# Attention with the softmax weights left unnormalised, and the outputs of two heads divided by rows of their sums

## The chip, the core and the metric

The kernel runs on one core of one Trainium2 chip. The metric is device time in microseconds (us) of one execution of the whole program; the number compared is the median of several. The core has a matrix engine (TensorE, in rows PE, its weight loads PEld), a vector engine (DVE), an activation engine (ACT), GpSimd (POOL) and a queue that only issues transfers (SP). They run side by side, each through its own queue of instructions in order, and wait for one another on semaphores.

## The reference

Two transformer blocks on 1024 tokens of width 1024. The first is a gated delta-net layer with an MLP. The second has, on the same input, softmax attention and a gated linear recurrence, then an output product and a gated MLP. The change is in the attention of the second block:

```
keys = concat([kc, kx])        # 256 context tokens + 1024 tokens = 1280 keys
vals = concat([vc, vx])
# 8 query heads of 64, 2 key/value heads, blocks of 128 queries
s = einsum('bqkgd,bnkd->bkgqn', q, keys) * scale
p = softmax(s, axis=-1)                       # exp(s - max) / sum
o = einsum('bkgqn,bnkd->bqkgd', p, vals)
```

The division by the sum is by query and head, so it may stand before or after the product with the values.

## The kernel before

All matrix products keep fp32 accuracy: each operand is split into a rounded part (`hi`) and a remainder (`lo`), and three (or two) products are added in PSUM.

`attention` works in chunks. A chunk is 128 queries of one head against all 1280 keys. `chunks` lists 64 of them: head pair j (4), half of the tokens i (2), head of the pair h (2), block of 128 queries c (4). So one (j, i) is eight chunks: two heads, four blocks. Two chunks that follow each other make a pair m (32 pairs).

For one chunk `dots` issues six matmuls into a PSUM tile called `logits` (four banks of 512 columns; even chunks use columns 0 to 1279, odd ones 768 to 2047, so that neighbours overlap). DVE takes the row maximum (line 1248). `rest` is the exponential on ACT (line 1252), which writes the weights `w` (128 x 1280) and, by `accum_out`, their sum into a small tile `st`. `norm` is a reciprocal on DVE (line 1255) and a multiplication of the whole tile `w` by it on POOL (line 1256).

The loop over `steps` takes a pair in five steps s of 256 keys. A step turns four 128 x 128 pieces of the pair's two `w` tiles on PE into a PSUM tile from `k.pt()` (line 1336; there are two such buffers), ACT rounds that to `ph` (line 1340), DVE makes the remainder `pl` (line 1345), and `product` multiplies both by the values into `pv` (lines 1323, 1324), three steps later or so. In step 0 of pair m the dots of chunk 2m+3 are issued, in step 2 those of chunk 2m+4; their exponentials follow in the same step, and their `norm` one step later. The pieces of chunk 2m+3 are first turned in step 0 of the next pair. At the end of four chunks `tail` adds the two halves of `pv` (ACT copy to `ao`, line 1266, DVE add to `att`, line 1267). After the second head (h = 1) it sends `att` to memory, or, for j = 3, splits it into `mixed[3]` (lines 1272, 1273).

Into this loop other work is put by `fill`: the projection of the next queries and their norm and rotation (`prep`, whose multiplications are on POOL, lines 1114 to 1129), and a gate (`gate`). In the last fifth, results of the other heads are read back and split on POOL (`split_mixed`, line 1381).

The order on each engine is not simply that of the program. The framework has a planner that takes instructions by their place in the program when their inputs are ready by its own modelled durations, and writes the queues down before the kernel runs. So PE turns the pieces of the pair's first chunk earlier than those of the second where the second comes later, and a `w_out` load of the following stage is issued while the attention has just begun. On the chip each queue is then followed strictly.

After the loop comes the output product (`out_tile`, line 2057): eight tiles over the first half of the tokens, then eight over the second. `mixed[3]` is its last operand.

Of the kernel before, what the change touches and what calls it, by code (L numbers as in the profile page):

```python
# [9 lines left out]
F32 = mybir.dt.float32  # L10
F32R = mybir.dt.float32r
AF = mybir.ActivationFunctionType
ALU = mybir.AluOpType
AX = mybir.AxisListType
# [179 lines left out]
def drain(g):  # L194
    for _ in g or ():
        pass
# [832 lines left out]
def mixer(k, hhi, hlo, mixd, cpd):  # L1029

    nc, tc = k.nc, k.tc
    w_in = k.A["w_in_2"]

    def proj(n, evac, o=0):
        W = k.wload(w_in[:, 128 * n:128 * n + 128])
        for i, sl in enumerate(HALVES):
            ps = k.pg()
            k.gemm(ps, W, hhi, hlo, sl)
            evac(ps, slice(o + 512 * i, o + 512 * i + 512), i)

    k.nh = (hhi, hlo)
    mixed = [None] * 8
    with tc.tile_pool(name="mix", bufs=1, reuse_waits="tile") as P:
        with tc.tile_pool(name="hgr", bufs=1, reuse_waits="tile") as R:
            first = Keys(k, P, cpd)
            hgrn(k, P, R, proj, mixd, cpd, first)
        with tc.tile_pool(name="att", bufs=1, reuse_waits="tile") as R:
            attention(k, P, R, proj, mixd, cpd, mixed, first)
    return mixed
# [110 lines left out]
def attention(k, P, R, proj, mixd, cpd, mixed, first):  # L1160

    nc, A = k.nc, k.A
# [33 lines left out]
                nc.scalar.copy(v[:, :, 0:64], p)  # L1196
                nc.vector.tensor_tensor(out=v[:, :, 64:128], in0=p, in1=v[:, :, 0:64], op=ALU.subtract)

    QT, Q, W, att = {}, {}, {}, {}
    logits = k.psL.tile([128, 2048], F32, name="logits")  # L1200

    def prep(j):
# [23 lines left out]
    def queries(j, i):  # L1226


        ps = k.pt()
        for c in range(4):  # L1230
            nc.tensor.transpose(ps[:, 128 * c:128 * c + 128], QT[j][:, 4 * i + c, :], k.ident)
        for h in range(2):
            QS = Q[j, i, h] = R.tile([128, 512], F32R, tag="QS", name=k.nm("QS"), bufs=4)
            p, o = slice(64 * h, 64 * h + 64), slice(64 * (1 - h), 64 * (1 - h) + 64)
            nc.scalar.copy(QS[p, :], ps[p])
            nc.vector.tensor_tensor(out=QS[o, :], in0=ps[p], in1=QS[p, :], op=ALU.subtract)

    def dots(n):

        j, i, h, c = chunks[n]  # L1240
        g, q = j // 2, Q[j, i, h][:, 128 * c:128 * c + 128]
        o = 768 * (n % 2)
        lg = logits[:, o:o + 1280]
        for a, b in (((0, 512), (512, 1024), (1024, 1280)), ((768, 1280), (256, 768), (0, 256)))[n % 2]:
            nc.tensor.matmul(lg[:, a:b], q, KH[g][:, a:b], start=True, stop=False)
            nc.tensor.matmul(lg[:, a:b], q, KL[g][:, a:b], start=False, stop=True)
        st = R.tile([128, 4], F32, tag="st", name=k.nm("st"), bufs=4)
        nc.vector.tensor_reduce(out=st[:, 0:1], in_=lg, axis=AX.X, op=ALU.max, negate=True)
        w = W[n] = R.tile([128, 1280], F32, tag="w", name=k.nm("w"), bufs=5)

        def rest():
            nc.scalar.activation(w, lg, AF.Exp, bias=st[:, 0:1], accum_out=st[:, 1:2])

        def norm():
            nc.vector.reciprocal(st[:, 2:3], st[:, 1:2])  # L1255
            nc.gpsimd.tensor_scalar(w, w, st[:, 2:3], None, op0=ALU.mult)  # L1256
        return rest, norm

    def tail(j, i, h, pv):

        if h == 0:
            att[j, i] = R.tile([128, 512], F32, tag="att", name=k.nm("att"), bufs=2)
        o, sl = att[j, i], HALVES[i]
        p = slice(64 * h, 64 * h + 64)
        o2 = R.tile([64, 512], F32, tag="ao", name=k.nm("ao"), bufs=1)
        nc.scalar.copy(o2, pv[64:128, :])
        nc.vector.tensor_tensor(out=o[p, :], in0=pv[0:64, :], in1=o2, op=ALU.add)
        if h == 0:
            return
        if j == 3:  # L1270
            hi, lo = mixed[3]
            nc.scalar.copy(hi[:, sl], o)
            nc.gpsimd.tensor_tensor(out=lo[:, sl], in0=o, in1=hi[:, sl], op=ALU.subtract)
        else:
            nc.sync.dma_start(mixd[j][:, sl], o)

    def reload(f):

        mixed[f] = halves(f)
        nc.sync.dma_start(mixed[f][1].bitcast(F32), mixd[f])  # L1280

    def halves(f):
        return tuple(k.s2.tile([128, 1024], F32R, tag="s2", name=f"mx{c}{f}") for c in "hl")

    chunks = [(j, i, h, c) for j in range(4) for i in range(2) for h in range(2) for c in range(4)]
# [8 lines left out]
    def fill(n=1):  # L1294
        for _ in range(n):
            if todo:
                next(todo.pop(0), None)
                if not todo:
                    drain(fills[3])

    def ahead(n):
        return dots(n) if n < len(chunks) else (lambda: None, lambda: None)

    for n in range(3):
        rest, norm = ahead(n)
        rest()
        fill(3)
        norm()

    steps = [(m, s) for m in range(32) for s in range(5)]  # L1310
    waiting, pv = [], None
# [2 lines left out]
    def product(m, s, ph, pl):  # L1314

        nonlocal pv, hold
        j, i, h, c = chunks[2 * m]
        if c == 0 and s == 0:
            pv = k.psV.tile([128, 512], F32, tag="v", name=k.nm("pv"))
        out = pv[:, 128 * c:128 * c + 256]  # L1320
        for e in range(2):
            kt, sl = 2 * s + e, slice(256 * e, 256 * e + 256)
            nc.tensor.matmul(out, V[j // 2][:, kt, :], ph[:, sl], start=kt == 0, stop=False)
            nc.tensor.matmul(out, V[j // 2][:, kt, :], pl[:, sl], start=False, stop=kt == 9)
        if c == 2 and s == 4:
            tail(j, i, h, pv)
            hold = 2

    for n, (m, s) in enumerate(steps):
        if s == 0:  # L1330
            rest, norm = ahead(2 * m + 3)
        ps = k.pt()
        for e in range(2):
            for c in range(2):
                kt = 2 * s + e
                nc.tensor.transpose(ps[:, 256 * e + 128 * c:256 * e + 128 * c + 128],  # L1336
                                    W[2 * m + c][:, 128 * kt:128 * kt + 128], k.ident)
        ph = R.tile([128, 512], F32R, tag="ph", name=k.nm("ph"), bufs=4)
        pl = R.tile([128, 512], F32R, tag="pl", name=k.nm("pl"), bufs=4)
        nc.scalar.copy(ph, ps)  # L1340
        if s in (0, 2):
            if s == 2:
                rest, norm = ahead(2 * m + 4)
            rest()
        nc.vector.tensor_tensor(out=pl, in0=ps, in1=ph, op=ALU.subtract)  # L1345
        if s in (1, 3):
            norm()
        waiting.append((m, s, ph, pl))
        hold -= 1
        if hold < 0 or len(waiting) > 3:  # L1350
            for _ in range(2 if len(waiting) > 3 else 1):
                if len(waiting) > 2:
                    product(*waiting.pop(0))

        nxt = 2 * m + 6
        if s == 3 and nxt % 8 == 0 and nxt < len(chunks):
            j, i = chunks[nxt][:2]
            while j not in QT:
                fill()
            queries(j, i)  # L1360
        if n < 112 and (n * 83) // 108 != ((n + 1) * 83) // 108:
            fill()
        if n == 114:
            drain(fills[3])
            todo.clear()
            drain(fills[2])
            mixed[3] = halves(3)
        for f in {116: (4, 5), 122: (6, 7), 128: (0, 1), 134: (2,)}.get(n, ()):
            reload(f)
        if n in (130, 134, 138, 142, 146, 150, 154):  # L1370
            f = (4, 5, 6, 7, 0, 1, 2)[(n - 130) // 4]
            split_mixed(k, mixed[f], HALVES[0], nc.gpsimd.tensor_copy, nc.gpsimd)
# [5 lines left out]
def split_mixed(k, pair, sl, copy, eng=None):  # L1378
    hi, lo = pair[0][:, sl], pair[1][:, sl]
    copy(hi, lo.bitcast(F32))  # L1380
    (eng or k.nc.vector).tensor_tensor(out=lo, in0=lo.bitcast(F32), in1=hi, op=ALU.subtract)
# [789 lines left out]
```

## Time and profile before

| | us |
|---|---|
| median of 3 runs | 3133.63 (3132.91 to 3140.13) |
| profiled execution | 3129.6, of which the trace's span is 3127.8 |
| attention loop, first maximum to last product | about 1884 to 2325 in the span |
| PE busy in the span | 2840.2 (91%) |
| DVE, ACT, POOL busy in the span | 2131.3, 1402.3, 1075.1 |
| mean granted PE clock in the span | 0.961 |

Times in the rows are us from the start of the span unless they are marked ns. A row of a group of instructions has the source line, the engine, the operation, output<-input by the program's names, and a count; "idle before" is time in which the engine had nothing to do until the named instruction of another engine let it go. PEclk is the granted clock as a share of full speed.

### The profile page before, as it was taken

What the parts mean: (1) busy time and instruction counts of PE and PEld (TensorE: products, weight loads), DVE (VectorE), ACT (ScalarE), POOL (GpSimd) and SP (SyncE); (2) the same over time, 40 slices, a digit from 0 to 9 for tenths busy, and PEclk for the clock granted to TensorE, in tenths of its full rate; (3) what the DMA queues carried; (4) which work ended last, traced back from release to release, by engine and by line L of the source; (5) the groups of instructions that cost most, each with busy time, mean ns of one, the idle gap of its engine ahead of it and who ended that gap; (6) DMA issues with size and microseconds to landing.
All of it is one profiled execution on the core that took longest, in us unless ns stands there. A gap on an engine that the chain in (4) does not pass through costs nothing. (4 is left out here: it accounts for less than half of the span.)

```text
span 3127.8 us, 43961 instructions
## 1 busy us (share of the span) xinstructions
PE 2840.2 (91%) x16304; PEld 2313.7 (74%) x16304; DVE 2131.3 (68%) x3267; ACT 1402.3 (45%) x2677; POOL 1075.1 (34%) x756
## 2 busy tenths in 40 slices
PE   7899999997899989998999997787779899999998
PEld 5777777786677767887777776666667688887777
DVE  5777777737988699778566675555645855556784
ACT  6353535424555643345433335555434533334345
POOL 1101111005323464424322235656643433333432
PEclk9999999998999999999999998898989999999999
DMA  4313131222777654425311110001024333334333
GB/s 113 60 31 67 44 59 48 68 99 88 234 231 230 227 192 143 141 87 155 105 47 47 48 43 8 21 30 42 11 74 138 105 101 101 102 121 164 121 117 105
DMA packets 330086, 310.17 MB, mean 99 GB/s; under 512 B 36640, under 2 KB 254720, under 8 KB 329872
## 3 DMA queue, kind: packets, MB, share of 16 engines
q1 hardware_dynamic: 277088, 220.90, 23.1%
q10 hardware_dynamic: 46480, 65.46, 5.7%
q0 software_dynamic: 6304, 21.01, 3.0%
q8 instruction: 128, 2.10, 0.3%
q14 instruction: 86, 0.70, 0.1%
HBM read 232.83 MB, written 74.48 MB: 98 GB/s over the span
## 5 line engine op out<-in xcount | busy, mean ns | idle before, releaser
L1256 POOL TENSOR_SCALAR w<-w,st 128x1280 f32<-128x1280 f32 x64 | 225.2, 3519 | 181.9 <-DVE st L1255 173.4
L1703 PE MATMUL pt<-T,blk 128*128 128x512 f32 x608 | 241.8, 398 | 7.8 <-DVE e L2030 3.7
L1704 PE MATMUL pt<-T,blk 128*128 128x512 f32 x608 | 241.9, 398 | 3.7 <-DVE T L1780 3.7
L1705 PE MATMUL pt<-T,blk 128*128 128x512 f32 x608 | 241.2, 397 | 1.5 <-DVE blk L1692 1.5
L149 PE MATMUL pg<-dhi,whi 128*128 128x512 f32 (+1 forms) x528 | 214.0, 405 | 1.8 <-ACT pre L285 1.8
L150 PE MATMUL pg<-dlo,whi 128*128 128x512 f32 (+1 forms) x528 | 213.4, 404 | 0.9 <-DVE dlo L188 0.9
L139 ACT CAST whi<-wraw 128x1024 fp32r<-128x1024 f32 (+3 forms) x126 | 116.0, 921 | 219.0 <-PE pg L150 195.6
L151 PE MATMUL pg<-dhi,wlo 128*128 128x512 f32 (+1 forms) x528 | 212.8, 403 | 1.5 <-POOL wlo L140 1.5
L1336 PE MATMUL pt<-c_ident,w 128*128 128x128 f32 x640 | 123.0, 313 | 99.2 <-POOL w L1256 86.9
L1340 ACT CAST ph<-pt 128x512 fp32r<-128x512 f32 x160 | 91.7, 587 | 199.0 <-PE pt L1336 193.8
L1345 DVE TENSOR_TENSOR pl<-pt,ph 128x512 fp32r<-128x512 f32 x160 | 106.7, 686 | 105.1 <-ACT ph L1340 104.5
L1336 PEld LDWEIGHTS pt<-c_ident,w 128*128 128x128 f32 x640 | 85.2, 158 | 122.6 <-POOL w L1256 99.9
L1944 PE MATMUL pt<-T,blk 128*128 128x512 f32 x368 | 151.2, 411 | 24.8 <-DVE x L1951 17.4
L149 PE MATMUL pg<-xhi,whi 128*128 128x512 f32 x416 | 171.8, 413 | 1.4 <-ACT e L1025 1.4
L150 PE MATMUL pg<-xlo,whi 128*128 128x512 f32 x416 | 169.5, 407 | 0.0
L151 PE MATMUL pg<-xhi,wlo 128*128 128x512 f32 x416 | 169.1, 406 | 0.3 <-DVE wlo L140 0.3
L140 DVE TENSOR_TENSOR wlo<-wraw,whi 128x1024 fp32r<-128x1024 f32 (+3 forms) x101 | 111.1, 1100 | 76.5 <-ACT whi L139 71.7
L1945 PE MATMUL pt<-T,blk 128*128 128x512 f32 x368 | 149.4, 406 | 0.0
L1946 PE MATMUL pt<-T,blk 128*128 128x512 f32 x368 | 149.2, 406 | 0.0
L1703 PEld LDWEIGHTS pt<-T,blk 128*128 128x128 f32 x608 | 115.3, 190 | 37.6 <-DVE e L2030 4.1
L1692 DVE TENSOR_TENSOR blk<-xb,blk 128x512 fp32r<-128x512 f32 x121 | 102.6, 849 | 54.2 <-ACT blk L1691 52.5
L1704 PEld LDWEIGHTS pt<-T,blk 128*128 128x128 f32 x608 | 115.5, 190 | 31.9 <-DVE T L1780 5.3
(544 smaller groups left out, 8478.5 us busy)
## 6 DMA issues: line engine op xcount, KB each, us to landing
x<-w_mod SPq DMA_DIRECT2D x72, 256.0 KB
wraw<-w_in SPq DMA_DIRECT2D x35, 512.0 KB
T<-td SPq DMA_DIRECT2D x69, 256.0 KB
wraw<-dn_w_in SPq DMA_DIRECT2D x32, 512.0 KB
td<-e ACTq DMA_DIRECT2D x55, 256.0 KB
xb<-w_gu SPq DMA_DIRECT2D x44, 256.0 KB
wraw<-w_gu SPq DMA_DIRECT2D x22, 512.0 KB
xin<-x SPq DMA_DIRECT2D x16, 512.0 KB
```

The lines of the kernel that those rows point to most:

```text
L139: nc.scalar.copy(hi, raw)
L149: nc.tensor.matmul(out, hi[:, w, :], Hhi[k][:, sl], start=first and k == 0, stop=False)
L150: nc.tensor.matmul(out, hi[:, w, :], Hlo[k][:, sl], start=False, stop=False)
L151: nc.tensor.matmul(out, lo[:, w, :], Hhi[k][:, sl], start=False, stop=last and k == n - 1)
L1256: nc.gpsimd.tensor_scalar(w, w, st[:, 2:3], None, op0=ALU.mult)
L1336: nc.tensor.transpose(ps[:, 256 * e + 128 * c:256 * e + 128 * c + 128], W[2 * m + c][:, 128 * kt:128 * kt + 128], k.ident)
L1703: nc.tensor.matmul(ps, w[:, 0, j], T[j][:, 0], start=not c and j == 0, stop=False, skip_group_check=c)
L1704: nc.tensor.matmul(ps, w[:, 0, j], T[j][:, 1], start=False, stop=False, skip_group_check=c)
L1705: nc.tensor.matmul(ps, w[:, 1, j], T[j][:, 0], start=False, stop=j == 3, skip_group_check=c)
L1944: nc.tensor.matmul(ps, w[:, 0, j], T[j][:, 0], start=not c and j == 0, stop=False, skip_group_check=c)
L1945: nc.tensor.matmul(ps, w[:, 0, j], T[j][:, 1], start=False, stop=False, skip_group_check=c)
L1946: nc.tensor.matmul(ps, w[:, 1, j], T[j][:, 0], start=False, stop=j == n - 1, skip_group_check=c)
```

## The change

The weights `w` stay what the exponential gives. The reciprocal and the POOL multiplication of each chunk (64 of each) go. The exponential writes its sum into a column of one tile `sums` per (j, i), 128 queries by four blocks and two heads. Once per (j, i), eight times in all, `scales` is called in step 3 of its last pair: a reciprocal of the eight columns on DVE, a copy on POOL that repeats each of them 64 times (128 x 512), four transposes on PE into a `k.pt()` buffer, and a copy on ACT to `rows_`. `tail`, after the second head, multiplies the 128 x 512 outputs of both heads by these rows, on POOL and for the last group on DVE; there the remainder of `mixed[3]` moves from POOL to DVE too. In the start, the exponentials of the first three chunks are issued after three pieces of other work and not ahead of them.

```diff
-        st = R.tile([128, 4], F32, tag="st", name=k.nm("st"), bufs=4)
-        nc.vector.tensor_reduce(out=st[:, 0:1], in_=lg, axis=AX.X, op=ALU.max, negate=True)
+        top = R.tile([128, 1], F32, tag="top", name=k.nm("top"), bufs=2)
+        nc.vector.tensor_reduce(out=top, in_=lg, axis=AX.X, op=ALU.max, negate=True)
         w = W[n] = R.tile([128, 1280], F32, tag="w", name=k.nm("w"), bufs=5)
-        def rest():
-            nc.scalar.activation(w, lg, AF.Exp, bias=st[:, 0:1], accum_out=st[:, 1:2])
-        def norm():
-            nc.vector.reciprocal(st[:, 2:3], st[:, 1:2])
-            nc.gpsimd.tensor_scalar(w, w, st[:, 2:3], None, op0=ALU.mult)
-        return rest, norm
+        if (j, i) not in sums:
+            sums[j, i] = R.tile([128, 4, 2], F32, tag="sums", name=k.nm("sums"), bufs=2)
+        return lambda: nc.scalar.activation(w, lg, AF.Exp, bias=top, accum_out=sums[j, i][:, c, h:h + 1])
+
+    def scales(j, i):
+        r = sums[j, i]
+        nc.vector.reciprocal(r, r)
+        rows_[j, i] = w = R.tile([128, 512], F32, tag="rows", name=k.nm("rows"), bufs=1)
+        nc.gpsimd.tensor_copy(w.rearrange("p (c h d) -> p c h d", h=2, d=64), r.unsqueeze(3).to_broadcast([128, 4, 2, 64]))
+        ps = k.pt()
+        for c in range(4):
+            nc.tensor.transpose(ps[:, 128 * c:128 * c + 128], w[:, 128 * c:128 * c + 128], k.ident)
+        nc.scalar.copy(w, ps)
...
         if h == 0:
             return
+        last = j == 3 and i == 1
+        (nc.vector if last else nc.gpsimd).tensor_tensor(out=o, in0=o, in1=rows_[j, i], op=ALU.mult)
         if j == 3:
             hi, lo = mixed[3]
             nc.scalar.copy(hi[:, sl], o)
-            nc.gpsimd.tensor_tensor(out=lo[:, sl], in0=o, in1=hi[:, sl], op=ALU.subtract)
+            (nc.vector if last else nc.gpsimd).tensor_tensor(out=lo[:, sl], in0=o, in1=hi[:, sl], op=ALU.subtract)
...
     for n in range(3):
-        rest, norm = ahead(n)
+        rest = ahead(n)
+        fill(3)
         rest()
-        fill(3)
-        norm()
...
         nc.vector.tensor_tensor(out=pl, in0=ps, in1=ph, op=ALU.subtract)
-        if s in (1, 3):
-            norm()
+        if s == 3 and m % 4 == 3:
+            scales(*chunks[2 * m][:2])
```

## Rows read from the trace of the kernel before

**Rows 1.** Windows: busy us and (x) of each engine, PEclk, DMA share, GB/s.

```profile
1884.00:2325.00 441.00, 330.37 (x1882) 278.42 (x1881) 247.16 (x339) 221.34 (x359) 273.46 (x103) 0.88 0.06 20
2500.00:2700.00 200.00, 200.00 (x866) 162.65 (x865) 111.38 (x145) 71.97 (x124) 61.59 (x42) 1.00 0.31 101
```

**Rows 2.** Waits in 1880 to 2330: total us, times, longest.

```profile
ACT ph L1340 <- PE pt L1336: 193.8, 90, 10.8
...
PE pt L1336 <- POOL w L1256: 86.9, 40, 6.9
...
PE pt L1336 <- DVE pl L1345: 11.4, 23, 1.5
```

**Rows 3.** Groups by line in 1880 to 2330: busy us, mean ns of one.

```profile
L1256 POOL TENSOR_SCALAR w<-w,st 128x1280 f32<-128x1280 f32 x64 | 225.2, 3519 | 181.9 <-DVE st L1255 173.4 <-PE pv L1324 5.5 <-PE pt L1336 3.0
...
L1345 DVE TENSOR_TENSOR pl<-pt,ph 128x512 fp32r<-128x512 f32 x160 | 106.7, 686 | 105.1 <-ACT ph L1340 104.5
...
L1340 ACT CAST ph<-pt 128x512 fp32r<-128x512 f32 x160 | 91.7, 587 | 199.0 <-PE pt L1336 193.8 <-POOL gz L1223 2.8 <-issue 1.2
...
L1255 DVE RECIPROCAL st<-st 128x1 f32<-128x1 f32 x64 | 10.4, 162 | 37.7 <-ACT w L1252 37.5
...
L1114 POOL TENSOR_TENSOR qt<-qt,nss 128x1024 f32<-128x1024 f32 x3 | 5.7, 1902 | 0.5 <-DVE nss L203 0.5
...
L1380 POOL CAST mxh<-mxl 128x512 fp32r<-128x512 f32 x7 | 5.1, 745 | 0.0
```

**Rows 4.** Timeline of two chunks: start us, us, engine; then [idle before <-releaser].

```profile
2100.65 1.33 ACT L1252 ACTIVATE w<-logits,st 128x1280 f32<-128x1280 f32 x1
2102.11 0.16 DVE L1255 RECIPROCAL st<-st 128x1 f32<-128x1 f32 x1 [0.63 <-ACT w L1252]
2102.30 0.40 PE L1245 MATMUL logits<-KH,QS 128*128 128x512 f32 x1
2102.44 3.52 POOL L1256 TENSOR_SCALAR w<-w,st 128x1280 f32<-128x1280 f32 x1 [1.41 <-DVE st L1255]
2103.74 1.49 DVE L1248 TENSOR_REDUCE st<-logits 128x1 f32<-128x1280 f32 x1 [1.47 <-PE logits L1246]
2106.01 0.87 PE L1336 MATMUL pt<-c_ident,w 128*128 128x128 f32 x6 [2.03 <-POOL w L1256]
...
2106.65 1.07 ACT L1340 CAST ph<-pt 128x512 fp32r<-128x512 f32 x2 [3.90 <-PE pt L1336]
...
2107.61 1.34 ACT L1252 ACTIVATE w<-logits,st 128x1280 f32<-128x1280 f32 x1
...
2112.51 1.33 ACT L1252 ACTIVATE w<-logits,st 128x1280 f32<-128x1280 f32 x1
```

**Rows 5.** Timeline, the fourth exponential and the last of 64 (start us, us).

```profile
1908.03 1.34 ACT L1252 ACTIVATE w<-logits,st 128x1280 f32<-128x1280 f32 x1
...
2311.35 1.34 ACT L1252 ACTIVATE w<-logits,st 128x1280 f32<-128x1280 f32 x1
```

**Rows 6.** Timeline, the end of the attention and the start of what follows.

```profile
2316.70 1.54 PE L1336 MATMUL pt<-c_ident,w 128*128 128x128 f32 x6 [3.79 <-POOL w L1256]
...
2325.34 0.39 PE L149 MATMUL pg<-mxh,whi 128*128 128x512 f32 x1
2325.54 0.58 ACT L1266 COPY ao<-pv 64x512 f32<-64x512 f32 x1 [1.44 <-PE pv L1324]
...
2327.58 1.28 POOL L1273 TENSOR_TENSOR mxl<-att,mxh 128x512 fp32r<-128x512 f32 x1 [10.93 <-ACT mxh L1272]
```

**Rows 7.** Timeline of POOL around the longest distance between two exponentials.

```profile
2015.96 1.33 ACT L1252 ACTIVATE w<-logits,st 128x1280 f32<-128x1280 f32 x1
...
2023.04 2.34 POOL L1129 TENSOR_TENSOR qt<-qt,qf 128x1024 f32<-128x1024 f32 x1
2025.35 3.52 POOL L1256 TENSOR_SCALAR w<-w,st 128x1280 f32<-128x1280 f32 x1
...
2030.98 1.34 ACT L1252 ACTIVATE w<-logits,st 128x1280 f32<-128x1280 f32 x1
```

More of the change, by code (lines that the diff above doesn't have):

```diff
@@ L1197, in values @@
                 nc.vector.tensor_tensor(out=v[:, :, 64:128], in0=p, in1=v[:, :, 0:64], op=ALU.subtract)
-    QT, Q, W, att = {}, {}, {}, {}
+    QT, Q, W, att, sums, rows_ = {}, {}, {}, {}, {}, {}
     logits = k.psL.tile([128, 2048], F32, name="logits")
@@ L1301, in ahead @@
     def ahead(n):
-        return dots(n) if n < len(chunks) else (lambda: None, lambda: None)
+        return dots(n) if n < len(chunks) else lambda: None
     for n in range(3):
-        rest, norm = ahead(n)
+        rest = ahead(n)
+        fill(3)
         rest()
-        fill(3)
-        norm()
     steps = [(m, s) for m in range(32) for s in range(5)]
@@ L1330, in attention @@
         if s == 0:
-            rest, norm = ahead(2 * m + 3)
+            rest = ahead(2 * m + 3)
         ps = k.pt()
@@ L1342, in attention @@
             if s == 2:
-                rest, norm = ahead(2 * m + 4)
+                rest = ahead(2 * m + 4)
             rest()
         nc.vector.tensor_tensor(out=pl, in0=ps, in1=ph, op=ALU.subtract)
-        if s in (1, 3):
-            norm()
+        if s == 3 and m % 4 == 3:
+            scales(*chunks[2 * m][:2])
         waiting.append((m, s, ph, pl))
```

## The prediction, made blind

> **What bounds the kernel now.** I read the shares of the page first. PE is busy 91% of the span and POOL 34%, so a POOL saving looks worthless. But the shares are means over stages, so the windows come next [rows 1]. In a later stage PE is busy all 200 us at full clock. In the attention it is busy 330.4 of 441 us at 0.88 of full clock, and POOL, at 273 us, is nearly as loaded. Here is a hole of 110 us in PE, and the clock is low too.
>
> The waits say who digs it [rows 2]: PE waits 86.9 us, 40 times, for the POOL multiplication of `w`, and only 11.4 us for the PSUM buffers of the turned pieces (`pl`). The 193.8 us of ACT behind PE is the same stall handed on: ACT has nothing to round while PE has nothing to turn.
>
> The timeline of two chunks shows the mechanism [rows 4]. An exponential starts at 2100.65; reciprocal 2102.11; POOL 2102.44 for 3.52 us, done at 2105.96; PE, idle for 2.03 us, turns pieces at 2106.01; ACT rounds two of them from 2106.65, and only then does the next exponential start, at 2107.61, though its maximum was ready at 2103.74 + 1.49 = 2105.23. That gap is 6.96 us. The gap after it has no POOL wait in it and is 2112.51 - 2107.61 = 4.90 us. Through the whole loop the two kinds alternate: from the fourth exponential to the last are 60 gaps in 2311.35 - 1908.03 = 403.3 us, mean 6.72 [rows 5]; counting them off, the 30 gaps like the first have a mean of 8.03, the 30 like the second 5.42. So a softmax chunk costs 6.72 us, and a chunk free of the POOL pass about 5.
>
> **The change, step by step.**
>
> *Removed: 64 POOL multiplications* (64 x 3519 ns = 225 us) *and 64 reciprocals* (64 x 162 ns = 10.4 us) [rows 3]. Of the 225 us only what PE waits for counts: 86.9 us at most by the waits. What is late next is the chain of one chunk, without POOL: exponential and the reading of its sum to the next dots 2102.30 - 2100.65 = 1.65, dots to maximum 2103.74 - 2102.30 = 1.44, maximum 1.49, a hand-over [rows 4]. That is 4.6, and the neighbouring `logits` chunks overlap in PSUM, so it cannot be shorter without another layout; 4.90 is what a clear gap takes. With five roundings a pair in between (587 ns on ACT, 686 on DVE [rows 3]) and the projections, tails and queries that also stand in these queues, some gaps will be longer, as they are in the kind that has no POOL wait (mean 5.42, which includes gaps with PE at the low clock). I take 5.30 for all, between 4.90 and 5.42 and nearer to the second, because it already has that other work in it. Saving: 60 x (6.72 - 5.30) = 85.2 us. Bounds: 4.90 gives 109; 5.80 (more crowding, since nothing spreads the five steps any more) gives 55. The sum of the waits, 86.9, points to the same place from another view.
>
> *The end of the loop.* After the last exponential PE waits 3.79 us for the last POOL pass [rows 6]: -3.8.
>
> *The clock.* Of the 0.88 I book nothing apart: where it is low, dots and pieces take longer, and that is inside the mean of 5.42 from which I come down a little. If PE kept full clock throughout, the gaps would go toward 4.90, which is the lower bound above.
>
> *Added: `scales`, eight times.* On its way: reciprocal of eight columns (about 0.2, from 162 ns for one column), hand-over 0.17 (as 2102.27 to 2102.44 [rows 4]), the POOL copy, four transposes, an ACT copy of 128 x 512 (587 ns [rows 3]). The trace has no POOL copy that repeats a column. Below: a POOL cast of 128 x 512, 745 ns. Above: the 128 x 1280 multiplication by element, 3519 x 512/1280 = 1408 ns. The nearest in form is line 1114, which reads a small tile spread over 64 columns: 1902 ns for 1024 columns, so 0.95 for 512 [rows 3], which I take. Transposes: six took 0.87 [rows 4], so four 0.6. Together 2.5 us a group; most of it lies beside the chain, because the sums of a group are complete a whole pair before `scales` is called (the pair's second chunk got its exponential in step 0 of the pair before). On the path I count ACT's 0.59 and PE's 0.6, and one of the two `k.pt()` buffers being held meanwhile: 1.2 us a group, 9.4 in all. Bounds: 0 (hidden in the chain's slack), and 2.5 plus a DVE queue of one maximum ahead of the reciprocal (1.49), 4.0, so 32 in all, if PE reaches the transposes in its queue before the copy is done and everything behind them (pieces, products, dots) stands. The planner sets this place by its modelled times, which I can't read from rows.
>
> The Trainium skill, "GPSIMD Engine Reference", section 4.1, calls one-input operations on POOL roughly line-rate. At its 1.2 GHz the copy would be an estimated 0.43 us and the eight groups some 4 us shorter in latency. The trace speaks against it for the pass removed here (one tensor input, 2.75 ns an element [rows 3]); the sum goes by the rows.
>
> *Added: the multiplication in `tail`.* Seven on POOL, each like line 1273 (1.28 [rows 6]), between the add and a store that nobody in the loop awaits, on a POOL with 225 us less to do: 0. For (3, 0) ACT's copy of `hi` waits for POOL (about 1.5 us of ACT, once): inside the rounding of 9.4. If that cover is gone, at most 8 x 1.5 = 12, inside the bound above. The last is on DVE (about 0.69, line 1345's size), as is the remainder after it, which took 1.28 on POOL. This end isn't awaited: the output product starts at 2325.34, before `tail`'s first copy at 2325.54, on the first half of the tokens, and eight tiles come before the half that `tail` writes [rows 6].
>
> *Moved: the first three exponentials behind `fill(3)`.* They pass the matmuls, one weight rounding and one evacuation of `prep` in ACT's queue, and SP's weight load. PE is busy with these projections anyway; against it stands that the first POOL pass goes. I put it at +1, between -3 and +6.
>
> *Sum*: -85.2 - 3.8 + 9.4 + 1 = -78.6. Against the profiled execution, 3129.6, that is 3051.0. The median of the runs is 3133.6, 4.0 more, so the forecast on that scale is **3055**. After the loop PE is the bound at full clock [rows 1] and starts earlier by as much; nothing there waits for the clock on the wall.
>
> **The rivals.**
>
> *The floor*: all gaps come down to 4.90 and `scales` hides but for 5 us. -109 - 3.8 + 5 = -108: 3026. For it: the clear gaps are in the trace. Against: the mean of their kind is 5.42.
>
> *Below the floor*: dots start under the exponential. The first 512 columns that a chunk writes are in a bank which the chunk before doesn't touch, so its first two matmuls (2102.30 to 2102.77, 0.47 us [rows 4]) could run earlier; gaps of 4.43 give 60 x 2.29 = 137, + 3.8 - 9 = 132: 3002. Against: dots start after the end of the exponential before in every one of the chunks. The Trainium skill, "PSUM — Partial Sum Buffer", section "PSUM bank collisions raise a hardware error", asks for guards by bank and not by address or tile, so by that rule this overlap is open; the trace doesn't use it, and nothing in the change makes the planner use it.
>
> *Crowding*: without the POOL wait the steps pile up on two buffers, gaps of 5.80, and `scales` costs 3.5 a group: -55 - 3.8 + 28 = -31: 3103. For it: five roundings and two exponentials fill 6 of 9.8 us of ACT a pair, and each blocks the other in a strict queue.
>
> *Slower*: the transposes of `scales` stand in PE's queue while POOL still works through the rotation of the next queries. The trace has such a case [rows 7]: line 1129 and its sisters hold back one multiplication until 2025.35, and the gap between exponentials is 15.0, some 10.1 more than a clear one. If each group paid that and its own 2.5, 8 x 12.6 = 101 against 89 gained: +12, 3146. It decides from 89/8 = 11.1 a group. Against: there are only three such rotations and seven splits for eight groups, and POOL is otherwise empty then.
>
> *No change*: the PE hole is only renamed, waits for `pl` growing as those for POOL go: 3134. Against: 4.90 beside 6.96 in one timeline.
>
> **Chances.** Forecast (3030 to 3085) 0.58, floor 0.16, below it 0.04, crowding 0.13, no change 0.04, slower 0.05. About 0.3%, 9 us, can be told from no change here. Faster: 0.58 + 0.16 + 0.04 + 0.13 = 0.91, less 0.02 for crowding that goes further: 0.89; same 0.05; slower 0.06. The range takes in the floor and most of crowding, and leaves out what lies below and the last two: 3022 to 3100.
>
> **What would show it.** Right: no wait of PE for POOL in the loop but for the eight row copies; gaps between exponentials near 5.3 of both kinds; attention some 360 us long in place of 441; granted clock there over 0.92; POOL near 65 us (273 - 225 + 8 x 0.95 + 7 x 1.28). Wrong: gaps that stay over 6, with PE waiting for `pl` or ACT for the maximum; PE waits over 3 us ahead of the `rows` transposes; a later stage that grows by what this one lost.

## The result, and the profile after

The changed kernel takes 3023.5 us (median of 4, 3018.0 to 3032.5) where the one before takes 3136.9: ratio 0.9637, interval 0.9603 to 0.9671, so 113 us less. Two later comparisons gave 0.9634 (0.9615 to 0.9653) and 0.9620 (0.9604 to 0.9636). The forecast was 3055, 79 less than before: the sign and the place are right, the size is a third short. The rival called the floor (3026) came nearest, and 3023.5 lies outside the forecast's own interval of 3030 to 3085.

The attention by windows, after (busy us and count of PE, PEld, DVE, ACT, POOL; then PEclk, DMA share, GB/s), answers to [rows 1]:

```profile
1901.00:2231.00 330.00, 301.21 (x1937) 257.81 (x1936) 233.98 (x286) 225.93 (x369) 62.97 (x54) 0.99 0.09 29
2500.00:2700.00 200.00, 200.00 (x867) 162.61 (x866) 112.75 (x147) 72.94 (x125) 59.85 (x42) 1.00 0.32 105
```

The stretch has gone from some 441 to some 330 us. PE is busy 91% of it, at 0.99 of full clock where it had 0.88; POOL has 63 us left of 273. The later stage is as it was.

The waits, after (total us, times, longest), answer to [rows 2]:

```profile
ACT ph L1347 <- PE pt L1343: 73.4, 71, 2.0
...
PE pt L1343 <- DVE pl L1352: 15.9, 23, 1.5
...
PE logits L1245 <- ACT w L1252: 7.9, 15, 2.2
```

The 86.9 us of PE behind POOL are gone entirely, and no wait of PE for the row copies has come in their place. ACT's wait for pieces fell from 193.8 to 73.4. The wait for `pl` grew only from 11.4 to 15.9.

Three exponentials and the link between them, after, answer to [rows 4]:

```profile
2067.13 1.33 ACT L1252 ACTIVATE w<-logits,top 128x1280 f32<-128x1280 f32 x1
...
2068.60 0.50 PE L1245 MATMUL logits<-KH,QS 128*128 128x512 f32 x1
...
2070.07 1.49 DVE L1248 TENSOR_REDUCE top<-logits 128x1 f32<-128x1280 f32 x1 [0.31 <-PE logits L1246]
...
2071.59 1.33 ACT L1252 ACTIVATE w<-logits,top 128x1280 f32<-128x1280 f32 x1 [0.29 <-DVE top L1248]
...
2076.12 1.33 ACT L1252 ACTIVATE w<-logits,top 128x1280 f32<-128x1280 f32 x1 [0.56 <-DVE top L1248]
```

The gap is now 4.46 and 4.53 us, and what ACT waits for last is DVE's maximum and no longer PE's pieces. The reader can add it up: exponential to dots 1.47, dots to maximum 1.47, maximum 1.49. The fourth and the last exponential, against [rows 5], and what starts behind the loop, against [rows 6]:

```profile
1920.68 1.33 ACT L1252 ACTIVATE w<-logits,top 128x1280 f32<-128x1280 f32 x1
...
2217.23 1.34 ACT L1252 ACTIVATE w<-logits,top 128x1280 f32<-128x1280 f32 x1
```

```profile
2226.26 0.39 PE L149 MATMUL pg<-mxh,whi 128*128 128x512 f32 x1
```

Sixty gaps in 296.6 us are 4.94 each, for 6.72 before. Counted off by their parts from the timeline, 30 gaps of each kind, in us:

| | exp. to dots | dots | to max. | max. | max. to exp. | gap |
|---|---|---|---|---|---|---|
| before, with the POOL wait | 1.85 | 1.41 | 0.29 | 1.49 | 2.99 | 8.03 |
| before, without | 1.82 | 1.62 | 0.17 | 1.49 | 0.32 | 5.41 |
| after, the first kind | 1.51 | 1.41 | 0.18 | 1.49 | 0.38 | 4.97 |
| after, the second kind | 1.51 | 1.43 | 0.13 | 1.49 | 0.36 | 4.92 |

Most of it, 30 x 2.6 = 78 of the 107 us, is the time by which ACT let the first kind of exponential wait for pieces. The rest is mainly the 0.3 us from exponential to dots, in both kinds (20 us), and the slower dots of the second kind (6 us). The lower clock goes with the latter: during the dots of the second kind the granted clock was 0.88 on average before and 0.99 after. For the 0.3 us no run separates the clock from the work that had piled up in PE's queue.

The two profiled spans differ by 97.3 us: +17.0 ahead of the attention (the turning of the keys starts at 1872.9 and 1889.9, in queues that have not changed), -4.4 from the first to the fourth exponential beyond that, -106.8 in the gaps, -5.0 from the last exponential to the output product (13.99 to 9.03), +1.7 behind it. The attention alone is thus -116; the +17 is this execution's own, the slowest of the four, and no effect of the change shows in it: two other profiles of the same kernel start their first exponential at 1890.3 and 1896.2, where this has 1903.7.

### The profile page after: what moved, and what is told of

Read it like the earlier page. It is cut to its first block, busy times and chain, and to the rows that moved or that the text cites. A ratio compares the mean times of both kernels' runs of the same rounds, so it can differ in the third digit from the quotient of the medians.

```text
span 3030.5 us, 43838 instructions
## 1 busy us (share of the span) xinstructions
PE 2818.1 (93%) x16336; PEld 2297.5 (76%) x16336; DVE 2115.3 (70%) x3213; ACT 1407.0 (46%) x2685; POOL 861.5 (28%) x706
## 5 line engine op out<-in xcount | busy, mean ns | idle before, releaser
L1710 PEld LDWEIGHTS pt<-T,blk 128*128 128x128 f32 x608 | 115.4, 190 | 38.6 <-DVE e L2037 4.2
L1711 PEld LDWEIGHTS pt<-T,blk 128*128 128x128 f32 x608 | 115.5, 190 | 30.3 <-DVE T L1787 3.7
L1712 PEld LDWEIGHTS pt<-T,blk 128*128 128x128 f32 x608 | 115.3, 190 | 28.9 <-DVE blk L1699 2.3
L1935 ACT CAST blk<-T 128x384 fp32r<-128x384 f32 (+1 forms) x133 | 71.9, 541 | 140.5 <-PE pt L1953 80.9
L1899 ACT CAST T<-T 128x512 fp32r<-128x512 f32 x161 | 97.0, 619 | 81.5 <-DMA T<-td 41.9
L1711 PE MATMUL ps<-T,blk 128*128 128x512 f32 x304 | 123.5, 406 | 8.3 <-DVE T L1787 8.2
```

The lines of the kernel that those rows point to most:

```text
L1710: nc.tensor.matmul(ps, w[:, 0, j], T[j][:, 0], start=not c and j == 0, stop=False, skip_group_check=c)
L1711: nc.tensor.matmul(ps, w[:, 0, j], T[j][:, 1], start=False, stop=False, skip_group_check=c)
L1712: nc.tensor.matmul(ps, w[:, 1, j], T[j][:, 0], start=False, stop=j == 3, skip_group_check=c)
```

## Experiments

**Is it the pass, or its length?** The kernel before with the multiplication on DVE:

```diff
-            nc.gpsimd.tensor_scalar(w, w, st[:, 2:3], None, op0=ALU.mult)
+            nc.vector.tensor_scalar(w, w, st[:, 2:3], None, op0=ALU.mult)
```

> The kernel before, with the normalising multiplication of w on DVE and not on POOL; nothing else changes. The question is whether the pass itself was dear or only its 3.52 us on the way from the exponential to the pieces. A DVE multiplication of 128 x 1024 took 748 ns in this trace, so about 0.9 us for 128 x 1280. Theory A (the length of the pass held PE's pieces, and with them ACT's roundings and the next exponential): the wait from the maximum to the exponential of even chunks falls from 2.99 to below 0.7, the mean gap from 6.72 to about 5.3, time -75 to -95 us against before; the rest to the changed kernel (-113) is DVE's extra 0.9 + 0.16 us a chunk. Rival B (a pass over w costs, wherever it stands, since it must come between the exponential and the pieces): the gap stays over 6, less than -45 us.

Ratio 0.9680 (0.9661 to 0.9699): -100 us. The mean gap is 5.23, the wait from maximum to exponential 0.43 in both kinds. Theory A holds, a little beyond its -95. The pass, by line and engine (busy us, mean ns, idle before):

```profile
L1256 DVE TENSOR_SCALAR w<-w,st 128x1280 f32<-128x1280 f32 x64 | 60.9, 952 | 1.8
```

At 0.95 us it is short enough to hide: PE waits 1.6 us for it in the whole loop. One word of the old kernel gives most of what the whole change gives. The rest is some 13 us; it would fit the 61 us of passes and 10 us of reciprocals that this run leaves in DVE's queue and the change doesn't, but no run tests that alone.

**Would more lead do?** The kernel before, one chunk further ahead (and, for space, one buffer less of `att` and of `QS`):

```diff
-        w = W[n] = R.tile([128, 1280], F32, tag="w", name=k.nm("w"), bufs=5)
+        w = W[n] = R.tile([128, 1280], F32, tag="w", name=k.nm("w"), bufs=6)
...
-    for n in range(3):
+    for n in range(4):
...
-            rest, norm = ahead(2 * m + 3)
+            rest, norm = ahead(2 * m + 4)
...
-                rest, norm = ahead(2 * m + 4)
+                rest, norm = ahead(2 * m + 5)
```

> The kernel before, with every chunk's dots, maximum, exponential and POOL pass issued one chunk earlier (a sixth buffer of w; for its space att has one buffer and QS three). POOL does the same 225 us. Theory A (what cost was the lead, not POOL's work): PE's wait for POOL falls from 86.9 us to under 30 and the mean gap to 5.1 to 5.5: -70 to -95 us; bunches of rotation work on POOL still cost some. Rival B (POOL's throughput, 273 of 441 us busy, or its use of memory beside DVE is the price): under -35 us.

Ratio 0.9901 (0.9881 to 0.9922): -31 us. Theory A missed, and the numbers fall under its rival. But POOL isn't saturated either; it waits 137 us for reciprocals. The trace shows a third thing. Pieces turned (line 1336) and exponentials done, before up to 2106.00 and in this kernel up to 2096.10, each time the moment at which PE has waited for POOL:

```profile
1880.00:2106.00 226.00, 56.99 (x302) 40.11 (x302) 0.88 0.05 16
```

```profile
L1252 ACT ACTIVATE w<-logits,st x32: 1319/1332/1347, 1886.7 to 2100.6; 128x1280 f32<-128x1280 f32 x32
```

```profile
1880.00:2096.10 216.10, 52.19 (x301) 37.17 (x301) 0.92 0.06 18
```

```profile
L1252 ACT ACTIVATE w<-logits,st x32: 1322/1333/1346, 1892.4 to 2090.7; 128x1280 f32<-128x1280 f32 x32
```

Both have done 32 exponentials and are 30 chunks and a piece or two into the turning. The extra chunk that was issued at the start is no longer there. It was lost where the queues are written. In the program the edit puts every exponential one chunk sooner, that is two or three roundings. In ACT's queue, as the trace has it, the exponentials from the fourth on stand only 0.9 roundings sooner on average, and 25 of these 61 stand where they stood. The last one comes behind 155 roundings in the kernel before and in this one (counted up to 2311.30 and 2281.20, just ahead of it):

```profile
L1340 ACT CAST ph<-pt x155: 574/587/608, 1901.4 to 2310.9; 128x512 fp32r<-128x512 f32 x155
```

```profile
L1340 ACT CAST ph<-pt x155: 565/587/612, 1906.7 to 2280.7; 128x512 fp32r<-128x512 f32 x155
```

So the planner gave most of the lead back, and in 23 of this kernel's 33 waits for POOL no more exponentials were done ahead of the pieces than before. The run shows what this edit brings; what a queue that kept the lead would bring, it doesn't show. At such a wait:

```profile
2090.74 1.33 ACT L1252 ACTIVATE w<-logits,st 128x1280 f32<-128x1280 f32 x1
...
2092.53 3.52 POOL L1256 TENSOR_SCALAR w<-w,st 128x1280 f32<-128x1280 f32 x1 [1.63 <-DVE st L1255]
...
2096.10 0.55 PE L1336 MATMUL pt<-c_ident,w 128*128 128x128 f32 x3 [1.78 <-POOL w L1256]
...
2096.74 0.59 ACT L1340 CAST ph<-pt 128x512 fp32r<-128x512 f32 x1 [1.90 <-PE pt L1336]
2097.23 1.33 ACT L1252 ACTIVATE w<-logits,st 128x1280 f32<-128x1280 f32 x1
```

The same order as in [rows 4]: exponential, pass, pieces, rounding, next exponential. So these five make one closed path where the rounding stands ahead of the next exponential in ACT's queue.

**Does a shorter way to the first pieces help?** That was put to the test on the kernel before, with POOL's work unchanged in place and a little larger:

```diff
-            nc.gpsimd.tensor_scalar(w, w, st[:, 2:3], None, op0=ALU.mult)
+            for a in (0, 640):
+                nc.gpsimd.tensor_scalar(w[:, a:a + 640], w[:, a:a + 640], st[:, 2:3], None, op0=ALU.mult)
```

> The kernel before, with the POOL pass over w in two halves by keys (columns 0 to 639, then 640 to 1279), so that the pieces of the first two steps wait only for the first half. One such half took 1.9 us in the run with a free POOL; POOL's work grows from 225 to 244 us and stays in its place. In the early run PE still waited 71 us for POOL, about 2 us each time, though every chunk had a chunk more lead. Theory A (chunks are made more slowly than they are used, so PE always stands at the newest one, and exponential, pass, pieces and rounding make one path to the next exponential; lead can't help, a shorter way to the first pieces can): the even chunks' wait from maximum to exponential falls from 2.99 to about 1.4, PE's wait for POOL under 40 us, -45 to -75 us. Rival B (the queue order is laid for a pass of another length and the miss of about 2 us stays whatever the pass takes): PE's wait over 60 us, -25 us or less.

Ratio 0.9843 (0.9811 to 0.9874): -49 us, inside A and out of B. The first kind's wait from maximum to exponential fell from 2.99 to 2.06 and not to the 1.4 expected. (The lead that this expectation speaks of, every chunk a chunk ahead, was mostly not in the queues, as the run above shows. The edit here doesn't depend on it.) A typical wait of PE fell from 2.0 to 0.8:

```profile
2096.48 0.98 PE L1337 MATMUL pt<-c_ident,w 128*128 128x128 f32 x7 [0.82 <-POOL w L1257]
```

In all PE still waits 48.3 us, over the 40 expected, because the long waits of 3.2 to 5.7 us stay, where POOL is in a bunch of other work, as in [rows 7]. Together with the DVE run (pass 0.95 us, on another engine: -100) and the full pass (3.52 us: 0) this is a dose and its response.

**Does POOL's work cost by itself?** The changed kernel with the old amount of work for POOL, whose results nobody reads:

```diff
...
+        junk = R.tile([128, 640], F32, tag="junkw", name=k.nm("junkw"), bufs=1)
+        spare.append(lambda: [nc.gpsimd.tensor_scalar(junk, w[:, a:a + 640], k.ones, None, op0=ALU.mult) for a in (0, 640)])
...
-        nc.gpsimd.tensor_copy(w.rearrange("p (c h d) -> p c h d", h=2, d=64), r.unsqueeze(3).to_broadcast([128, 4, 2, 64]))
+        nc.vector.tensor_copy(w.rearrange("p (c h d) -> p c h d", h=2, d=64), r.unsqueeze(3).to_broadcast([128, 4, 2, 64]))
...
+        if s in (1, 3) and spare:
+            spare.pop(0)()
...
```

> The changed kernel, with POOL multiplying every w by ones into a scratch tile that nobody reads, in two halves, at the places of the old pass; the copy to rows and the multiplication in tail are on DVE so that nothing waits for POOL there (att one buffer, QS three, for space). POOL has its 225 us back, the chain is free of it. Theory A (the wait counts, not the work): within 10 us of the changed kernel, so -100 to -115 against before. Rival B (POOL's traffic slows its neighbours): maxima above 1.49 us or pl above 0.69 us in the trace and 20 us or more of the gain gone.

Ratio 0.9690 (0.9672 to 0.9708): -97 us. POOL did 244 us of it in the loop, and 97 of some 114 us of the gain stay, so most of what the old pass cost was not POOL's work as such. The 17 that go were not expected by A. B's mechanism isn't in the trace: the maximum took 1486 ns (1489 in the changed kernel), `pl` 684 (683). The trace shows where about half of the 17 went. POOL was not wholly without someone who waits: the gate's product (line 1223) now stands behind multiplications into the scratch tile, and ACT, which has to send it to memory, waits for it:

```profile
2000.19 5.84 POOL L1253 TENSOR_SCALAR junkw<-w,c_ones 128x640 f32<-128x640 f32 x3
2005.99 1.26 POOL L1223 TENSOR_TENSOR gz<-gz 128x512 f32<-128x512 f32 x1
```

```profile
2007.65 0.58 ACT L1235 CAST QS<-pt 64x512 fp32r<-64x512 f32 x1 [9.20 <-POOL gz L1223]
```

This gap between exponentials is 12.17 us, 6.5 more than the same one in the changed kernel; at the second such product ACT waits 3.3 us, and the gap is 3.1 longer. So POOL's load does cost where something on the path stands behind it in POOL's queue. For the rest there are the row copies and multiplications that moved to DVE (8 x 793 and 8 x 688 ns, 11.8 us of its queue); how much of it is theirs is open.

**What does the added part cost?** The changed kernel without `scales` and without the multiplication in `tail` (the division is left out), beside the changed kernel itself:

```diff
-        if s == 3 and m % 4 == 3:
-            scales(*chunks[2 * m][:2])
...
-        (nc.vector if last else nc.gpsimd).tensor_tensor(out=o, in0=o, in1=rows_[j, i], op=ALU.mult)
```

> The changed kernel once more, unchanged, as the base of the three beside it: 0.9637 of before, 3024 us where before is 3137; in the trace a mean gap between exponentials of 4.9 to 5.0 us.

> The changed kernel without scales and without the multiplication in tail: the division by the sums is left out, all else is as it was. It prices the added part. My forecast put it at 9.4 us (1.2 a group on the path). Theory A (the chain of the chunks has room beside it: PE 92% and ACT 71% busy in the loop, and nobody was seen to wait for the rows): 0 to 4 us faster than the changed kernel. Rival B (it takes its own time on ACT and PE, and a buffer): 8 to 12 us faster.

With the rows 0.9634 (0.9615 to 0.9653), without 0.9625 (0.9611 to 0.9638): 3019.9 and 3019.2 us. The difference is 0.7 us, with some 7 us of uncertainty either way; A holds. The groups of the added part in the changed kernel fit this (busy us, mean ns, idle before):

```profile
L1259 POOL COPY rows<-sums 128x512 f32<-128x512 f32 x8 | 4.9, 615 | 140.3 <-DVE sums L1257 140.3
L1262 PE MATMUL pt<-c_ident,rows 128*128 128x128 f32 x32 | 4.8, 274 | 0.6 <-DVE pl L1352 0.5
L1263 ACT COPY rows<-pt 128x512 f32<-128x512 f32 x8 | 4.7, 590 | 0.9 <-PE pt L1262 0.8
```

In this trace PE never waits for the copy: the planner put the transposes behind it. ACT's copies, I infer, take time that ACT would have spent waiting for the maximum.

**Does the start matter?** The changed kernel with the exponentials ahead of the fills:

```diff
-        fill(3)
-        rest()
+        rest()
+        fill(3)
```

> The changed kernel with the first three exponentials ahead of their fill(3), as before. My forecast put the move at +1 us. In the two traces the stretch from the first exponential to the fourth is 21.3 us before and 16.9 us after, 4.4 less, but there the POOL pass is gone too. Theory A (the removed POOL pass made that gain, and the place of the exponentials makes none): within 2 us of the changed kernel. Rival B (the move made it): 3 to 6 us slower.

Ratio 0.9619 (0.9606 to 0.9633), 3017.8 against 3019.9 us: the place of the exponentials makes no difference, as A said. First to fourth exponential takes 16.9 us here too, so what the start gained came from the missing POOL pass.

**What binds now?** Two probes of the chain. First, every maximum taken twice:

```diff
-        nc.vector.tensor_reduce(out=top, in_=lg, axis=AX.X, op=ALU.max, negate=True)
+        for _ in range(2):
+            nc.vector.tensor_reduce(out=top, in_=lg, axis=AX.X, op=ALU.max, negate=True)
```

> The changed kernel, with the row maximum of every chunk taken twice (the second one is the same result). Theory A (the changed loop is bound by the chain exponential - dots - maximum of one chunk after the other, 1.51 + 1.42 + 0.15 + 1.49 + 0.37 = 4.94 us): each gap grows by 1.49 less the slack of about 0.3, to 6.1 to 6.4; +70 to +95 us on the changed kernel, -18 to -43 against before. Rival B (it is bound by PE, 92% busy in the loop): DVE has 25% of its time free and takes it up; less than +30 us, so more than -83 against before.

Ratio 1.0075 (1.0054 to 1.0097), +135 us on the changed kernel (3158.4 against about 3023), more than A's 95. The gap is 7.14: 2.2 more for 1.49 us added. Two things come on top. Between the two maxima DVE mostly does a `pl` (in 45 of the 60 gaps), so that the second starts 0.5 us after the first ends. And PE's granted clock fell while PE stood idle more, as the window shows, and dots took 1.74 for 1.42:

```profile
1891.00:2355.00 464.00, 358.36 (x1916) 298.14 (x1915) 320.61 (x346) 228.71 (x365) 63.14 (x54) 0.86 0.06 20
```

Then a link taken shorter, the maximum over 1024 of the 1280 keys:

```diff
-        nc.vector.tensor_reduce(out=top, in_=lg, axis=AX.X, op=ALU.max, negate=True)
+        nc.vector.tensor_reduce(out=top, in_=lg[:, 0:1024], axis=AX.X, op=ALU.max, negate=True)
```

> The changed kernel with the maximum that is subtracted taken over the first 1024 of the 1280 keys. Softmax doesn't change by what is subtracted, and with these inputs the left-out keys exceed it by at most 75, so nothing overflows; for other inputs that would not be safe, so this is a probe of the chain and no version to keep. It shortens one link, the maximum, by a fifth (1.49 to about 1.2 us), and takes work from DVE alone. Theory A (after the change the chain exponential - dots - maximum still sets the gap): the mean gap falls from 4.94 by 0.2 to 0.4, 12 to 24 us faster than the changed kernel, so 0.956 to 0.960 of before. Rival B (PE, 92% busy in the loop, or the crowding of the roundings sets it): less than 8 us faster.

> The changed kernel unchanged, as the base beside it: 0.9634 of before.

0.9582 (0.9569 to 0.9595) beside 0.9620 (0.9604 to 0.9636): 3007.6 and 3020.3, so -12 to -13 us, at the near end of A, with some 6 us of uncertainty either way:

```profile
L1248 DVE TENSOR_REDUCE top<-logits 128x1 f32<-128x1024 f32 x64 | 78.0, 1219 | 17.5 <-PE logits L1246 16.8
```

The link lost 0.27 us, the gap 0.15 (4.94 to 4.80), less than the 0.2 to 0.4 that A expected. With the doubled maximum beside it, the chain still binds, but about half of what it is relieved of is lost again; that it goes into the queue of PE, busy 93% of that stretch, is likely and not shown.

**Can the next dots start under the exponential?** The changed kernel with each exponential in two pieces, the shared banks first:

```diff
...
+        parts = ((512, 1280), (0, 512)) if n % 2 == 0 else ((0, 768), (768, 1280))
...
+            for t, (a, b) in enumerate(parts):
+                nc.scalar.activation(w[:, a:b], lg[:, a:b], AF.Exp, bias=top, accum_out=sums[j, i][:, t, c, h:h + 1])
...
```

> The changed kernel with each exponential in two pieces, first the columns in the two PSUM banks that the next chunk shares, then those of its own bank (two partial sums, added once per group; att has one buffer for space). Theory A (the chain binds, and dots wait for the exponential only where they share a bank): the next dots can start some 0.5 us earlier, the gap falls from 4.94 to 4.6 or 4.7 until PE is the bound: 10 to 20 us faster than the changed kernel. Rival B (dots wait for the whole exponential whatever bank it reads): the second piece adds its fixed cost, gaps grow by 0.2 to 0.4, 12 to 25 us slower.

Ratio 0.9677 (0.9663 to 0.9690), 3034.5 against 3019.9: +15 us. B holds. The dots follow the end of the second piece, here in the rows of ACT and then of PE. In none of the 60 gaps do they start sooner than 0.05 us after the reading of the second sum, and in 43 of them the trace names the exponential as what released them. A part of the 15 may come from the single `att` buffer, for which PE waits 6.4 us here and not at all in the changed kernel:

```profile
2062.70 0.91 ACT L1256 ACTIVATE w<-logits,top 128x768 f32<-128x768 f32 x1
...
2063.59 0.69 ACT L1256 ACTIVATE w<-logits,top 128x512 f32<-128x512 f32 x1
2064.16 0.21 ACT L1256 ACTIVATION_READ_ACCUMULATOR w<-logits,top 128x1 f32 x1
```

```profile
2064.42 0.50 PE L1245 MATMUL logits<-KH,QS 128*128 128x512 f32 x1
```

None of the experiments is a version that is faster than the changed kernel and safe for all inputs.

## Why the prediction was right, and where its size was off

*The bound, right.* PE waited for POOL, ACT for PE, and so the next exponential. That is gone, and with it the low clock (0.88 to 0.99) and most of the hole in PE, which shrank from 111 us to 29. Of ACT's 193.8 us behind PE, which I called the same stall handed on, 73.4 stay without POOL, so 120 were that stall.

*The saving in the gaps, mis-sized.* I took 5.30 us for every gap; it is 4.94. The error is 60 x 0.36 = 22 us. I had argued that the kind without a POOL wait (5.42; to the second place it is 5.41) already held the other work that would remain. It held the stall too: its dots started 0.31 us later after the exponential and ran 0.19 us slower. A clear gap of 4.90 stood in [rows 4]; the mean beside it was contaminated by the thing to be removed. The sum of the waits, 86.9, seemed to confirm 85, and misled in the same way: it holds what PE lost while standing, and the gaps gave back 107, with the slower dots and the later starts of the table above.

*`scales`, mis-sized.* I booked 9.4 us (eight times 0.59 + 0.6 is 9.5); it costs none that can be measured. ACT and PE seem to have room for it while the maximum is on DVE. The copy took 615 ns, below my 745 to 1408, that is 1.2 ns an element, where the multiplication by a column took 2.75. The Trainium skill, "GPSIMD Engine Reference", section 4.1, calls one-input operations roughly line-rate, by which the prediction's estimate for the copy was 0.43 us; the copy came nearer to that than the multiplication, and for both the measurement decides.

*The start*, booked at +1 with bounds of -3 and +6, was -4.4, and the runs show that the pass and not the moved exponentials did it. *The end*, booked at -3.8, was -5.0.

Together 22 + 9.4 + 5.4 + 1.2 = 38 us short of the -116 in the trace, from a forecast of -79. That the time still lies in the range, 1.5 us above its lower end of 3022, is owed to the floor, which the range took in with a chance of 0.16, and not to the forecast's own sum: there all four terms leaned the same way.

*The rivals.* The floor (gaps of 4.90, `scales` nearly hidden) was the better forecast. "Below the floor" asked that dots start under the exponential; the split run shows that they wait for all of it, also where they write a bank that it doesn't read. The rule in the Trainium skill ("PSUM — Partial Sum Buffer", section "PSUM bank collisions raise a hardware error") asks for guards by bank and not by address. The wait in the trace is coarser than that, so it comes from how the program is synchronised; whether by tile or for another reason is open. "Crowding" shows only as 0.4 to 0.5 us over the shortest gap, 4.45. "Slower" didn't come: PE's wait for the row copies is not in the rows at all. Nor did "no change": the wait for `pl` grew by 4.5 us where 86.9 went.

## What to carry to other kernels

A pass between a producer and its consumer costs by its length where the consumer's work stands ahead of the producer's next step in a strict queue; a shorter pass on another engine or a scaling put off until after the product takes it off the path. An earlier issue in the program brought 31 of the 113 us here, and the queues that the planner wrote had given most of the lead back: look in the trace whether such a lead is still there. When the time of a stage without a stall is wanted, take the clear intervals of the trace and not the mean of those beside the stall. A linear scaling that can follow a product belongs behind it, where it is done once a group and the engines have room.

## What the runs showed of the hardware that I had not expected

POOL's cost depends on the form: 2.75 ns an element for a multiplication of a 128 x 1280 tile by a column (3519 ns), 1.2 for a copy that repeats a column (615 ns for 512). The same multiplication took DVE 952 ns. Doubling a link of 1.49 us cost 2.2 us a gap, not 1.49: 0.5 of it was other work of DVE between the two, and dots grew from 1.42 to 1.74 us with PE's granted clock down from 0.99 to 0.86 over the stretch. POOL's 244 us of multiplications beside them left the maximum (1486 and 1489 ns) and `pl` (684 and 683 ns) as they were.
